# The second score matmul of two 64-wide attentions with 128 contraction rows instead of 64

## Chip, core and metric

The kernel runs on one core of a Trainium2 chip. Five engines work side by side, each through its own queue in a fixed order: TensorE (PE, with the weight loads PEld), VectorE (DVE), ScalarE (ACT), GpSimd (POOL) and SyncE (SP, which issues the DMAs here). The metric is the time of one execution on the device in microseconds (us), the median of several runs.

## What is computed

Three transformer blocks follow each other on one sequence of 1024 positions and width 1024, in float32. The change concerns the first and the third. The first block has differential attention with 4 heads; each head has two maps of width 64, a linear bias and a causal mask:

```python
scores = jnp.einsum('bhmqd,bhmkd->bhmqk', qblk, kt) + bias[None, :, None]
p = jax.nn.softmax(scores, axis=-1)
a = p[:, :, 0] - lam * p[:, :, 1]
return jnp.einsum('bhqk,bhkv->bhqv', a, vt)
```

Beside it runs a chunked retention, then an output projection and a feed-forward layer. The second block is convolutional and local. The third has attention over a window of 128 positions with 8 query heads of width 64, 2 key heads and a sink:

```python
s = jnp.einsum('bnqhgd,bnkhd->bnhgqk', qb, kw).astype(jnp.float32) * (D ** -0.5)
s = jnp.where(allowed[None, :, None, None], s, -jnp.inf)
p = jax.nn.softmax(jnp.concatenate([s, sink], axis=-1), axis=-1)[..., :-1]
```

and beside it a gated linear recurrence (HGRN2), cross-attention to a memory, and a convolutional feed-forward layer.

## The kernel before

**Number format.** PE multiplies in the format float32r, which keeps fewer bits than float32. So operands are split in a hi part, which ACT writes (`split`, L143), and a lo part, the rest, which DVE or POOL writes (L145). A product is three matmuls into one PSUM bank: hi x hi, hi x lo, lo x hi (`mm3`, L178 to L180). `dense` runs that over 8 slices of the contraction, 24 matmuls of 512 columns, `dense_tm` with 256 columns.

**Scores with width 64.** A contraction has 128 rows, a map only 64. The kernel uses that. For map m, `qs[m]` holds the query's hi part in the map's own 64 rows and its lo part in the other 64; `ks[m]` holds the key's hi part twice. One matmul with 128 rows then gives hi x hi + lo x hi. The term hi x lo is left: a second matmul into the same bank takes the 64 rows of `qs[m]` with the hi part, and the same 64 rows of `kl`, in which the lo parts of both maps lie one below the other. In the first block that pair is L539 and L540 in `attn_diff`, with operands from `proj_diff` (ACT writes at L458 and L463, DVE at L459 and L464, and four DMAs that carry parts to the other 64 rows). In the third block it is L1459 and L1460 in `window`, with operands from `stack`.

**First block, order of work.** For each head i: `attn_diff(i)`, the projections of the retention (`proj_ret`), the score operands of the next head (`proj_diff(i + 1)`), the retention (`attn_ret`), the next values (`proj_v`). Within `attn_diff`, pairs of 128 queries run over at most two column pieces of up to 512 keys: 24 score pairs a head. DVE adds the bias and takes the maximum (L544), ACT takes the exponential (L550), DVE combines both maps (L560), PE transposes (L568), ACT and DVE split the result (L570, L571), and PE multiplies by the values (`ps_o`). ACT copies that out (L576), and `finish` norms it: column sums on PE (L204), a power on POOL (L217), spreading on PE (L237).

**Third block.** There are 8 units, one for each of 4 head pairs and 2 halves of the sequence. In each, the steps of `core` (the recurrence: matmuls L1548, copies L1549, outputs L1559), of `window` (4 pieces of 128 queries, two heads each: 8 score pairs) and of the next unit's projections (`proj`) are interleaved.

**What sets the order.** Each engine's order is set when the kernel is built, by the framework's scheduler. It takes instructions in an order of its own from what their inputs, their tile buffers and its own estimates allow. PE then works strictly through the list. Most large tiles come from one pool of 37 slots (`SLOTS`, `e.slot`); a tile that finds no free slot waits until the last reader of an older one is done. PSUM banks are few: after `psum_split(d=2, s=3)` the attention has two for dense sums, three for scores, two for transposes and one for outputs (`ps_o`).

Of the kernel before, what the change touches and what calls it, by code (L numbers as in the profile page):

```python
# [10 lines left out]
F32 = mybir.dt.float32  # L11
F32R = mybir.dt.float32r
U8 = mybir.dt.uint8
AF = mybir.ActivationFunctionType
ALU = mybir.AluOpType
# [4 lines left out]
T = 1024  # L20
# [8 lines left out]
def half(h):  # L29
    return slice(h * HALF, h * HALF + HALF)  # L30


def blk(i, n=P):
    return slice(i * n, i * n + n)
# [325 lines left out]
def block1(e, next_gain):  # L360


    nc, tc, io = e.nc, e.tc, e.io
# [42 lines left out]
    with ExitStack() as c2:  # L406
# [38 lines left out]
        def proj_diff(hd):  # L445

            scale = 0.125 * 2.0 ** (2 * (hd + 1))
            ts = [e.slot("qk", (T,), F32R) for _ in range(5)]
            qs, ks, kl = ts[0:2], ts[2:4], ts[4]
            wq = e.chunk(io["w1_fm"][hd])  # L450
            wk = e.chunk(io["w1_fm"][4 + hd])
            for h in range(2):
                sl = half(h)
                ql = e.tsq(dt=F32R)
                p = normed(e.dense(wq, hs[h]), h)
                for m in range(2):
                    b = slice(64 * m, 64 * m + 64)
                    nc.scalar.activation(qs[m][b, sl], p[b], AF.Copy, scale=scale)  # L458
                    nc.vector.scalar_tensor_tensor(ql[b], p[b], scale, qs[m][b, sl].bitcast(F32), op0=ALU.mult, op1=ALU.subtract)  # L459
                p = normed(e.dense(wk, hs[h]), h)  # L460
                for m in range(2):
                    b = slice(64 * m, 64 * m + 64)
                    nc.scalar.activation(ks[m][b, sl], p[b], AF.Copy)  # L463
                    nc.vector.tensor_tensor(kl[b, sl], p[b], ks[m][b, sl].bitcast(F32), op=ALU.subtract)  # L464
                for m in range(2):
                    b = slice(64 * m, 64 * m + 64)
                    o = slice(64 - 64 * m, 128 - 64 * m)
                    nc.sync.dma_start(qs[m][o, sl].bitcast(F32), ql[b].bitcast(F32))
                    nc.sync.dma_start(ks[m][o, sl].bitcast(F32), ks[m][b, sl].bitcast(F32))
            return qs, ks, kl  # L470
# [47 lines left out]
        def attn_diff(hd, ops, v):  # L518
            qs, ks, kl = ops
            vh, vl = v  # L520
            slope = 2.0 ** (-2 * (hd + 1))
            for pr in range(4):
# [6 lines left out]
                for i in range(2):  # L529
                    qb = 2 * pr + i  # L530
                    sums = e.small.tile([P, 2, 2], F32, tag="sums", name="sums")
                    pm = []
                    for m in range(2):
                        mx = None
                        pc = []
                        for c, n in cols:
                            s = e.pss()[:, :n]
                            b = slice(64 * m, 64 * m + 64)
                            nc.tensor.matmul(s, lhsT=qs[m][:, blk(qb)], rhs=ks[m][:, c : c + n], start=True, stop=False)  # L539
                            nc.tensor.matmul(s, lhsT=qs[m][b, blk(qb)], rhs=kl[b, c : c + n], start=False, stop=True)  # L540
                            mx2 = e.small.tile([P, 1], F32, tag="mx", name="mx", bufs=8)
                            st = c - qb * P + 896
                            pt = pring.next()[:, :n]
                            nc.vector.tensor_tensor_reduce(  # L544
                                pt, s, strip[:, st : st + n], scale=-slope,
                                scalar=BIG if mx is None else mx, op0=ALU.add, op1=ALU.min, accum_out=mx2)
                            mx = mx2
                            pc.append(pt)
                        for j, pt in enumerate(pc):
                            nc.scalar.activation(pt, pt, AF.Exp, bias=mx, scale=-1.0, accum_out=sums[:, j, m : m + 1])  # L550
                        pm.append(pc)

                    if len(cols) == 2:
                        nc.vector.tensor_tensor(sums[:, 0], sums[:, 0], sums[:, 1], op=ALU.add)
                    rs = e.small.tile([P, 2], F32, tag="rs", name="rs")
                    nc.vector.reciprocal(rs, sums[:, 0])
                    nc.vector.tensor_copy(pre[:, qb % 4 : qb % 4 + 1], rs[:, 0:1])
                    nc.vector.scalar_tensor_tensor(rs[:, 1:2], rs[:, 1:2], nlam, sums[:, 0, 0:1], op0=ALU.mult, op1=ALU.mult)
                    for p0, p1 in zip(*pm):
                        nc.vector.scalar_tensor_tensor(p0, p1, rs[:, 1:2], p0, op0=ALU.mult, op1=ALU.add)  # L560
                    aa.append(pm[0])
# [759 lines left out]
def block3(e, acc, hs, rest, out):  # L1321
# [39 lines left out]
    with ExitStack() as c2:  # L1361
# [10 lines left out]
        def stack(w, scale, h, qs, kl=None):  # L1372

            p = e.dense(w, hs[h])
            ql = e.tsq(dt=F32R) if kl is None else kl
            for m in range(2):
                b = slice(64 * m, 64 * m + 64)
                o = slice(64 - 64 * m, 128 - 64 * m)
                nc.scalar.activation(qs[m][b], p[b], AF.Copy, scale=scale)
                nc.vector.scalar_tensor_tensor(ql[b], p[b], scale, qs[m][b].bitcast(F32), op0=ALU.mult, op1=ALU.subtract)  # L1380
                nc.sync.dma_start(qs[m][o].bitcast(F32), (ql[b] if kl is None else qs[m][b]).bitcast(F32))

        v = {}

# [30 lines left out]


        ks = [e.slot(f"k{m}", (T,), F32R) for m in range(2)]
        kl = e.slot("kl", (T,), F32R)
        va = e.slot("va", (8, P))

        def window_kv(h):
            stack(e.chunk(io["w3_fm"][4]), 1.0, h, [k[:, half(h)] for k in ks], kl[:, half(h)])
            p = e.dense(e.chunk(io["w3_fm"][5]), hs[h])
            t = e.tnt()
            nc.scalar.activation(t, p, AF.Copy)
            tp = e.pt()
            for b in range(4):
                nc.tensor.transpose(tp[:, blk(b)], t[:, blk(b)], e.ident)
            nc.vector.tensor_copy(va[:, 4 * h : 4 * h + 4], tp.rearrange("p (a b) -> p a b", a=4))
# [14 lines left out]
        def window(g, h):  # L1444
            qs = ops[g, h][4]
            po = e.po()
            for j4 in range(4):
# [7 lines left out]
                es = e.small.tile([P, 2], F32, tag="es2", name="es2")  # L1455
                pr = prring.next()
                for m in range(2):
                    b = slice(64 * m, 64 * m + 64)
                    nc.tensor.matmul(s[m], lhsT=qs[:, m, blk(j4)], rhs=ks[m][:, k0 : k0 + wd], start=True, stop=False)  # L1459
                    nc.tensor.matmul(s[m], lhsT=qs[b, m, blk(j4)], rhs=kl[b, k0 : k0 + wd], start=False, stop=True)  # L1460
                    nc.vector.tensor_tensor_reduce(pr[:, m, :wd], s[m], swm[:, w0:], scale=-1.0,
                                                   scalar=nsink[:, 2 * g + m : 2 * g + m + 1], op0=ALU.add, op1=ALU.min,
                                                   accum_out=mx[:, m : m + 1])
# [355 lines left out]
```

## Time and profile before

| | before |
|---|---|
| median of 3 runs | 3494.2 us (3491.73 to 3495.17) |
| profiled execution, its own time | 3490.75 us |
| its span, first to last instruction | 3489.0 us |
| PE busy | 3329.4 us, 95% of the span |
| weight loads (PEld) busy | 2737.6 us, 78% |
| DVE, ACT, POOL busy | 1922.8, 1348.9, 894.9 us |
| granted TensorE clock, mean | 0.974 |

An engine's busy time is the union of its instructions' spans. For PE the ends of matmuls are modelled and overlap the next, so the time from one start to the next tells more. The granted clock is the share of full speed that PE was given; it has two levels, 1.2 and 2.4 GHz, so 0.94 is a mean of time at both. In the lists of waits, an engine's idle time is put down to what came last.

### The profile page before, as it was taken

Reading aid. Unit: us, or ns where it says so; the run is one execution under the profiler, and the core shown is the slowest. Engines: PE = TensorE matmul, PEld = TensorE weight load, DVE = VectorE, ACT = ScalarE, POOL = GpSimd, SP = SyncE. Lnnn points to the kernel's source line nnn. Section 1 sums busy time; section 2 is a strip of 40 time slices with the busy share of each in tenths; the row PEclk is TensorE's granted clock in tenths of the full one; section 3 lists DMA queues with packets and bytes.
Section 4 is the critical chain, followed back from the end, with each engine's and each line's share of the span. In section 5 each row is a group of like instructions: output and inputs, shape, how many; then the busy total and the mean of one; then the engine's idle time right before and its main releaser. Section 6 shows DMA issues by size and latency. Waiting matters only on the chain.

```text
span 3489.0 us, 43291 instructions
## 1 busy us (share of the span) xinstructions
PE 3329.4 (95%) x16510; PEld 2737.6 (78%) x16510; DVE 1922.8 (55%) x3463; ACT 1348.9 (39%) x2354; POOL 894.9 (26%) x577
## 2 busy tenths in 40 slices
PE   7999998999999999889999899999899999999997
PEld 6788877888888887677667778878887788888886
DVE  8566566622222238984777575776635771434346
ACT  4444453412211233333544455554443442313132
POOL 2000013401100113521334444435333430202021
PEclk8999999999999999999999999999999999999999
DMA  4112123211111114345644221224423321111114
GB/s 126 46 44 59 49 77 125 94 58 43 46 53 53 43 60 139 115 120 164 204 153 133 74 68 58 82 85 151 151 67 103 133 93 57 47 53 44 53 42 146
DMA packets 122431, 306.23 MB, mean 88 GB/s; under 512 B 17008, under 2 KB 25584, under 8 KB 122224
## 3 DMA queue, kind: packets, MB, share of 16 engines
q1 hardware_dynamic: 122224, 303.47, 27.1%
q8 instruction: 130, 2.13, 0.3%
q14 instruction: 77, 0.63, 0.1%
HBM read 256.23 MB, written 40.37 MB: 85 GB/s over the span
## 4 chain that ended last, share of the span: by engine, by line
PE 38%; DVE 6%; issue 3%; ACT 2%; POOL 1%; DMA 0%; DVEq 0%; POOLq 0%; ACTq 0%
PE ps_d L178 11%; PE ps_d L180 11%; PE ps_d L179 11%; PE ps_s L1548 1%; ACT whi L143 1%; DVE act L145 1%; DVE ssum L263 0%; POOL wlo L145 0%; PE ps_o L1482 0%; PE ps_t L204 0%; DVE hSA L1549 0%; DVE pr L1124 0%; PE ps_s L1460 0%; DVE nq L272 0%; PE ps_d L1559 0%
## 5 line engine op out<-in xcount | busy, mean ns | idle before, releaser
L180 PE MATMUL ps_d<-act,wlo 128*128 128x512 f32 x2272 | 894.2, 394 | 14.5 <-DVE wlo L145 13.2
L178 PE MATMUL ps_d<-act,whi 128*128 128x512 f32 x2272 | 895.6, 395 | 8.0 <-ACT whi L143 4.3
L179 PE MATMUL ps_d<-act,whi 128*128 128x512 f32 x2272 | 895.9, 394 | 3.0 <-DVE act L145 3.0
L143 ACT ACTIVATE whi<-raw 128x1024 fp32r<-128x1024 f32 (+2 forms) x394 | 387.4, 984 | 969.9 <-PE ps_d L179 854.3
L145 POOL TENSOR_TENSOR wlo<-raw,whi 128x1024 fp32r<-128x1024 f32 (+1 forms) x162 | 391.9, 2422 | 740.1 <-ACT whi L143 714.2
L180 PEld LDWEIGHTS ps_d<-act,wlo 128*128 128x128 f32 x2272 | 429.8, 189 | 109.6 <-DVE wlo L145 17.1
L178 PEld LDWEIGHTS ps_d<-act,whi 128*128 128x128 f32 x2272 | 430.0, 189 | 103.3 <-ACT whi L143 9.2
L179 PEld LDWEIGHTS ps_d<-act,whi 128*128 128x128 f32 x2272 | 429.9, 189 | 98.9 <-issue 6.5
L145 DVE TENSOR_TENSOR wlo<-raw,whi 128x1024 fp32r<-128x1024 f32 (+2 forms) x232 | 259.1, 1117 | 276.5 <-ACT whi L143 276.0
L180 PE MATMUL ps_d<-up,wlo 128*128 128x512 f32 x864 | 336.5, 389 | 0.0
L179 PE MATMUL ps_d<-up,whi 128*128 128x512 f32 x864 | 336.2, 389 | 0.0
L178 PE MATMUL ps_d<-up,whi 128*128 128x512 f32 x864 | 335.5, 389 | 0.0
L686 POOL TENSOR_TENSOR nt<-sq 128x512 f32<-128x512 f32 x64 | 83.5, 1305 | 556.0 <-ACT sq L684 555.1
L180 PE MATMUL ps_d<-mix,wlo 128*128 128x512 f32 x512 | 202.6, 396 | 2.9 <-POOL wlo L145 2.9
L178 PE MATMUL ps_d<-mix,whi 128*128 128x512 f32 x512 | 201.1, 399 | 3.3 <-DVE acc L643 2.1
L179 PE MATMUL ps_d<-mix,whi 128*128 128x512 f32 x512 | 203.0, 397 | 0.0
L180 PEld LDWEIGHTS ps_d<-up,wlo 128*128 128x128 f32 x864 | 162.2, 188 | 34.0 <-DVE wlo L145 0.3
L179 PEld LDWEIGHTS ps_d<-up,whi 128*128 128x128 f32 x864 | 162.2, 188 | 33.8
L178 PEld LDWEIGHTS ps_d<-up,whi 128*128 128x128 f32 x864 | 162.2, 188 | 33.7
L693 DVE TENSOR_TENSOR acc<-ps_d,acc 128x512 f32<-128x512 f32 x96 | 66.4, 692 | 203.9 <-PE ps_d L180 203.9
L217 POOL TENSOR_TENSOR rr<-rv,mhalf 128x4 f32<-128x4 f32 (+1 forms) x43 | 45.8, 1065 | 486.3 <-DVE rv L211 274.6
L178 PE MATMUL ps_d<-whi,act 128*128 128x256 f32 x512 | 151.8, 299 | 19.4 <-ACT act L388 12.6
(404 smaller groups left out, 5528.5 us busy)
## 6 DMA issues: line engine op xcount, KB each, us to landing
raw<-in_w_up SPq DMA_DIRECT2D x94, 512.0 KB, 3.3
raw<-in_w_fm SPq DMA_DIRECT2D x84, 512.0 KB, 3.6
raw<-in_w_out SPq DMA_DIRECT2D x42, 512.0 KB, 3.3
raw<-in_w_down SPq DMA_DIRECT2D x64, 320.0 KB, 3.0
xd<-acc SPq DMA_DIRECT2D x64, 256.0 KB, 2.4
acc<-xd SPq DMA_DIRECT2D x64, 256.0 KB, 5.5
raw<-in_w_down SPq DMA_DIRECT2D x32, 384.0 KB, 3.2
raw<-in_w_tm SPq DMA_DIRECT2D x22, 512.0 KB, 3.3
```

The costliest lines, as they stand in the source:

```text
L143: nc.scalar.activation(hi, src, AF.Copy)
L145: e.tensor_tensor(lo, src, hi.bitcast(F32), op=ALU.subtract)
L178: nc.tensor.matmul(out, lhsT=wh, rhs=xh, start=start, stop=False)
L179: nc.tensor.matmul(out, lhsT=wh, rhs=xl, start=False, stop=False)
L180: nc.tensor.matmul(out, lhsT=wl, rhs=xh, start=False, stop=stop)
L217: self.nc.gpsimd.tensor_tensor(r, v, self.mhalf.broadcast_to([P, n]), op=ALU.pow)
L686: nc.gpsimd.tensor_tensor(u, r, r, op=ALU.mult)
L693: nc.vector.tensor_tensor(acc[f][:, h], p, acc[f][:, h], op=ALU.add)
L1548: nc.tensor.matmul(s[:, blk(j, 64)], lhsT=x[:, blk(j)], rhs=xv[:, nb * j : nb * j + nb, 1], start=True, stop=True)
```

## The change

The key's lo parts get a tile for each map. In `kl[m]` the map's own 64 rows hold the lo part as before, and the other 64 rows are set to zero by a memset on POOL. The second score matmul then takes all 128 rows of `qs[m]` and of `kl[m]`. What the query's lo rows add is multiplied by zero. Columns, PSUM banks and the number of matmuls stay. `proj_diff` takes 6 slots in place of 5 for each head, with two memsets; the third block takes one slot more for its whole length, and two memsets.

```diff
--- before.py
+++ after.py
@@ -445,8 +445,10 @@
         def proj_diff(hd):
 
             scale = 0.125 * 2.0 ** (2 * (hd + 1))
-            ts = [e.slot("qk", (T,), F32R) for _ in range(5)]
-            qs, ks, kl = ts[0:2], ts[2:4], ts[4]
+            ts = [e.slot("qk", (T,), F32R) for _ in range(6)]
+            qs, ks, kl = ts[0:2], ts[2:4], ts[4:6]
+            for m in range(2):
+                nc.gpsimd.memset(kl[m][64 - 64 * m : 128 - 64 * m].bitcast(F32), 0.0)
             wq = e.chunk(io["w1_fm"][hd])
             wk = e.chunk(io["w1_fm"][4 + hd])
             for h in range(2):
@@ -461,7 +463,7 @@
                 for m in range(2):
                     b = slice(64 * m, 64 * m + 64)
                     nc.scalar.activation(ks[m][b, sl], p[b], AF.Copy)
-                    nc.vector.tensor_tensor(kl[b, sl], p[b], ks[m][b, sl].bitcast(F32), op=ALU.subtract)
+                    nc.vector.tensor_tensor(kl[m][b, sl], p[b], ks[m][b, sl].bitcast(F32), op=ALU.subtract)
                 for m in range(2):
                     b = slice(64 * m, 64 * m + 64)
                     o = slice(64 - 64 * m, 128 - 64 * m)
@@ -535,9 +537,8 @@
                         pc = []
                         for c, n in cols:
                             s = e.pss()[:, :n]
-                            b = slice(64 * m, 64 * m + 64)
                             nc.tensor.matmul(s, lhsT=qs[m][:, blk(qb)], rhs=ks[m][:, c : c + n], start=True, stop=False)
-                            nc.tensor.matmul(s, lhsT=qs[m][b, blk(qb)], rhs=kl[b, c : c + n], start=False, stop=True)
+                            nc.tensor.matmul(s, lhsT=qs[m][:, blk(qb)], rhs=kl[m][:, c : c + n], start=False, stop=True)
                             mx2 = e.small.tile([P, 1], F32, tag="mx", name="mx", bufs=8)
                             st = c - qb * P + 896
                             pt = pring.next()[:, :n]
@@ -1372,13 +1373,15 @@
         def stack(w, scale, h, qs, kl=None):
 
             p = e.dense(w, hs[h])
-            ql = e.tsq(dt=F32R) if kl is None else kl
+            if kl is None:
+                ql = e.tsq(dt=F32R)
             for m in range(2):
                 b = slice(64 * m, 64 * m + 64)
                 o = slice(64 - 64 * m, 128 - 64 * m)
                 nc.scalar.activation(qs[m][b], p[b], AF.Copy, scale=scale)
-                nc.vector.scalar_tensor_tensor(ql[b], p[b], scale, qs[m][b].bitcast(F32), op0=ALU.mult, op1=ALU.subtract)
-                nc.sync.dma_start(qs[m][o].bitcast(F32), (ql[b] if kl is None else qs[m][b]).bitcast(F32))
+                lo = ql[b] if kl is None else kl[m][b]
+                nc.vector.scalar_tensor_tensor(lo, p[b], scale, qs[m][b].bitcast(F32), op0=ALU.mult, op1=ALU.subtract)
+                nc.sync.dma_start(qs[m][o].bitcast(F32), (lo if kl is None else qs[m][b]).bitcast(F32))
 
         v = {}
 
@@ -1415,11 +1418,13 @@
 
 
         ks = [e.slot(f"k{m}", (T,), F32R) for m in range(2)]
-        kl = e.slot("kl", (T,), F32R)
+        kl = [e.slot(f"kl{m}", (T,), F32R) for m in range(2)]
+        for m in range(2):
+            nc.gpsimd.memset(kl[m][64 - 64 * m : 128 - 64 * m].bitcast(F32), 0.0)
         va = e.slot("va", (8, P))
 
         def window_kv(h):
-            stack(e.chunk(io["w3_fm"][4]), 1.0, h, [k[:, half(h)] for k in ks], kl[:, half(h)])
+            stack(e.chunk(io["w3_fm"][4]), 1.0, h, [k[:, half(h)] for k in ks], [k[:, half(h)] for k in kl])
             p = e.dense(e.chunk(io["w3_fm"][5]), hs[h])
             t = e.tnt()
             nc.scalar.activation(t, p, AF.Copy)
@@ -1455,9 +1460,8 @@
                 es = e.small.tile([P, 2], F32, tag="es2", name="es2")
                 pr = prring.next()
                 for m in range(2):
-                    b = slice(64 * m, 64 * m + 64)
                     nc.tensor.matmul(s[m], lhsT=qs[:, m, blk(j4)], rhs=ks[m][:, k0 : k0 + wd], start=True, stop=False)
-                    nc.tensor.matmul(s[m], lhsT=qs[b, m, blk(j4)], rhs=kl[b, k0 : k0 + wd], start=False, stop=True)
+                    nc.tensor.matmul(s[m], lhsT=qs[:, m, blk(j4)], rhs=kl[m][:, k0 : k0 + wd], start=False, stop=True)
                     nc.vector.tensor_tensor_reduce(pr[:, m, :wd], s[m], swm[:, w0:], scale=-1.0,
                                                    scalar=nsink[:, 2 * g + m : 2 * g + m + 1], op0=ALU.add, op1=ALU.min,
                                                    accum_out=mx[:, m : m + 1])
```

The extra slot also changes the order. In the rows below, numbers of lines after L445 are 1 to 4 higher in the changed kernel (L576 is L577, L463 is L465).

PE at the end of head 1's attention, before: the last output matmuls (`ps_o`, 256 columns, with the values vh and vl), then dense work of the next head's key projection (`ps_d`).

```order
L178 MATMUL ps_o<-probT,vh 128x256
L179 MATMUL ps_o<-probT,vh 128x256
L180 MATMUL ps_o<-probT,vl 128x256
L179 MATMUL ps_d<-act,whi 128x512
L180 MATMUL ps_d<-act,wlo 128x512
L178 MATMUL ps_d<-act,whi 128x512
```

Seventeen such dense matmuls stand there, and the retention's output matmuls, which go to the same bank `ps_o`, come behind them.

PE at the same place in the changed kernel:

```order
L180 MATMUL ps_o<-probT,vl 128x256
L178 MATMUL ps_o<-probT,vh 128x512
L179 MATMUL ps_o<-probT,vh 128x512
L180 MATMUL ps_o<-probT,vl 128x512
L178 MATMUL ps_o<-probT,vh 128x384
L179 MATMUL ps_o<-probT,vh 128x384
L180 MATMUL ps_o<-probT,vl 128x384
L178 MATMUL ps_o<-probT,vh 128x256
L179 MATMUL ps_o<-probT,vh 128x256
L180 MATMUL ps_o<-probT,vl 128x256
L204 MATMUL ps_t<-ones_r,ssum 128x1 x4
L178 MATMUL ps_d<-act,whi 128x512
```

The retention's output matmuls (512, 384 and 256 columns) now follow the attention's directly, and the key projection's second half, all 24 of its matmuls, has moved behind the column sums L204. The same holds at the ends of heads 0 and 2.

ACT at that place, before (`probT` is the transposed or decayed weight, `o` the attention's output, `qk` a score operand):

```order
L458 ACTIVATE qk<-ps_d 64x512
L143 ACTIVATE probT<-prob 128x384
L143 ACTIVATE probT<-prob 128x256
L458 ACTIVATE qk<-ps_d 64x512
L576 ACTIVATE o<-ps_o 128x256
L259 ACTIVATE ssum<-o 128x512
L143 ACTIVATE whi<-raw 128x1024
L463 ACTIVATE qk<-ps_d 64x512 x2
```

ACT there in the changed kernel:

```order
L143 ACTIVATE probT<-prob 128x384
L143 ACTIVATE probT<-prob 128x256
L465 ACTIVATE qk<-ps_d 64x512
L577 ACTIVATE o<-ps_o 128x256
L460 ACTIVATE qk<-ps_d 64x512
L259 ACTIVATE ssum<-o 128x512
L143 ACTIVATE whi<-raw 128x1024
L465 ACTIVATE qk<-ps_d 64x512
L597 ACTIVATE prob<-ps_t,dec 128x128 x4
L465 ACTIVATE qk<-ps_d 64x512
```

Two of the writes of the next head's key tiles (L465) now stand behind the copy of the attention's output, because one of the six tiles takes the slot of this head's values.

POOL from the first block's start to the first retention, before (L145 splits the input, L217 is the power of a norm, L512 the retention's gate):

```order
L145 TENSOR_TENSOR act<-nq,act 128x512 x8
L217 TENSOR_TENSOR rr<-rv,mhalf 128x4 x3
L512 TENSOR_TENSOR nt<-nt,gate 128x512
L217 TENSOR_TENSOR rr<-rv,mhalf 128x4
L512 TENSOR_TENSOR nt<-nt,gate 128x512
```

POOL there in the changed kernel:

```order
L451 MEMSET qk 64x1024 x2
L145 TENSOR_TENSOR act<-nq,act 128x512 x8
L217 TENSOR_TENSOR rr<-rv,mhalf 128x4
L451 MEMSET qk 64x1024 x2
L217 TENSOR_TENSOR rr<-rv,mhalf 128x4 x2
L514 TENSOR_TENSOR nt<-nt,gate 128x512
```

Each head's two memsets stand ahead of work that was there before; those of head 1 wait for the last score matmul of head 0, whose operands lay in their slots.

## Rows read from the trace of the kernel before

**Rows 1.** Busy time of each engine, clock and DMA in three stretches

```profile
core 0: us, PE busy (x) PEld busy (x) DVE busy (x) ACT busy (x) POOL busy (x), PEclk, DMA share, GB/s
72.00:107.00 35.00, 32.82 (x113) 21.31 (x113) 30.03 (x74) 19.67 (x48) 6.51 (x4) 0.84 0.14 40
107.00:513.00 406.00, 405.34 (x2201) 330.39 (x2201) 237.17 (x598) 182.03 (x396) 26.75 (x22) 0.99 0.18 55
1946.00:2352.00 406.00, 381.62 (x2231) 315.85 (x2229) 274.42 (x649) 228.09 (x452) 181.56 (x154) 0.94 0.21 70
```

**Rows 2.** Timeline of PE, first block: start, duration (us), line, rows*columns loaded, output

```profile
89.08 0.40 PE L539 MATMUL ps_s<-qk 128*128 128x512 f32 x1
89.40 0.50 PE L540 MATMUL ps_s<-qk 64*128 64x512 f32 x1
89.83 0.50 PE L179 MATMUL ps_d<-act,whi 128*128 128x512 f32 x1
90.17 0.40 PE L180 MATMUL ps_d<-act,wlo 128*128 128x512 f32 x1
90.41 0.39 PE L178 MATMUL ps_d<-act,whi 128*128 128x512 f32 x1
90.64 0.40 PE L179 MATMUL ps_d<-act,whi 128*128 128x512 f32 x1
```

**Rows 3.** Timeline of PE, third block, around one score pair

```profile
2172.24 0.28 PE L1459 MATMUL ps_s<-k,swq 128*128 128x256 f32 x1
2172.44 0.38 PE L1460 MATMUL ps_s<-kl,swq 64*128 64x256 f32 x1
2172.75 0.50 PE L179 MATMUL ps_d<-act,whi 128*128 128x512 f32 x1
2173.09 0.39 PE L180 MATMUL ps_d<-act,wlo 128*128 128x512 f32 x1
```

**Rows 4.** Timeline of PE, two plain matmuls of 256 columns

```profile
175.02 0.28 PE L178 MATMUL ps_d<-whi,act 128*128 128x256 f32 x1
175.14 0.28 PE L179 MATMUL ps_d<-wlo,act 128*128 128x256 f32 x1
```

**Rows 5.** Timeline of the weight loads around rows 2, in brackets idle time before

```profile
89.40 0.18 PEld L540 LDWEIGHTS ps_s<-qk 64*128 64x128 f32 x1 [0.36 <-issue]
89.83 0.19 PEld L179 LDWEIGHTS ps_d<-act,whi 128*128 128x128 f32 x1 [0.25 <-issue]
90.17 0.19 PEld L178 LDWEIGHTS ps_d<-act,whi 128*128 128x128 f32 x1
```

**Rows 6.** One line's instructions: L540 in 107 to 513, L1460 in all

```profile
L540 PE MATMUL ps_s<-qk x79: 379/497/792, 107.2 to 510.3; 64*128 64x512 f32 x55, 64*128 64x256 f32 x24
...
L1460 PE MATMUL ps_s<-kl,swq x64: 323/380/579, 1946.6 to 2350.0; 64*128 64x256 f32 x56, 64*128 64x128 f32 x8
```

**Rows 7.** Waits of PE in 107 to 513, then 1946 to 2352: us, times, longest

```profile
PE ps_s L600 <- ACT prob L596: 0.7, 3, 0.2
...
PE ps_d L1559 <- DVE hSA L1549: 6.3, 6, 1.9
```

**Rows 8.** Waits of DVE in 72 to 107, then in 1946 to 2352

```profile
DVE prob L544 <- PE ps_s L540: 3.2, 3, 2.3
...
DVE rv L207 <- PE ps_t L204: 29.5, 7, 9.7
DVE hSA L1549 <- PE ps_s L1548: 19.3, 15, 3.4
DVE pr L1461 <- PE ps_s L1460: 18.4, 9, 4.9
```

**Rows 9.** Timeline of ACT at the end of head 1; POOL's memset of the second block

```profile
290.45 0.39 ACT L576 ACTIVATE o<-ps_o 128x256 f32<-128x256 f32 x1
...
L875 POOL MEMSET cb<- x2: 942/952/962, 1406.1 to 1419.1; 128x1024 f32 x2
```

## Prediction

> **What bounds the kernel now.** I read first the busy times by stretch, then TensorE's own instructions around one score pair, then who waited for whom. The two attentions that change lie in 72 to 513 us (first block) and in 1946 to 2352 us (third block). In [rows 1] TensorE (PE) is busy 405.3 of 406 us from 107 to 513, with the vector engine (DVE) at 237 us: nothing but PE limits that stretch. In 72 to 107 PE has 32.8 of 35 us, but DVE 30.0: both are near their limit. In 1946 to 2352 PE has 381.6 of 406 us, DVE 274.4, ACT 228.1, and the granted clock is 0.94, against 0.99 in the long stretch before.
>
> "Busy" hides the point, since a matmul's end is modelled; start-to-start times show it. In [rows 2] the first score matmul of a pair (L539, 128 rows, 512 columns) starts at 89.08, the second (L540, 64 rows) at 89.40, the next one with 128 rows at 89.83, the one after at 90.17 and two more at 90.41 and 90.64. So the intervals are 0.32, 0.43, 0.34, and then 0.24 and 0.23 between matmuls that all have 128 rows. The same at 256 columns in the third block is in [rows 3]: 0.20, 0.31, 0.34, where [rows 4] gives 0.12 from one 256-column matmul to the next. The weight loads tell why: the load for the 64-row matmul starts only with it, after 0.36 us in which the load path waits for nothing that the profile shows ("issue"), and so does the load of the next 128-row matmul (0.25); the load after that has no such gap [rows 5]. A change of the row count on PE, in either direction, thus stops the overlap of the next load with the running matmul.
>
> **The change, part by part.**
>
> *The second score matmul with 128 rows.* It has as many columns as before, and the number of columns sets PE's time: 0.23 us at 512, 0.12 at 256. Its extra rows multiply zeros. Both changes of row count beside each pair go. Per 512-column pair followed by a 512-column matmul: 0.32 + 0.43 + 0.34 = 1.09 becomes 3 x 0.23 = 0.69, a gain of 0.40 [rows 2]. Per 256-column pair: 0.20 + 0.31 + 0.34 = 0.85 becomes 0.12 + 0.12 + 0.23 = 0.47, a gain of 0.38 [rows 3, 4]. There are 79 pairs in 107 to 513 and 64 in the third block [rows 6], and 96 - 79 = 17 earlier (24 pairs a head, four heads).
>
> *107 to 513 us.* 79 x 0.40 = 31.6 us. What hides it? Nothing: PE waits 0.7 us for others in the whole stretch [rows 7], and DVE is at 58%. I take all of it.
>
> *72 to 107 us.* 17 x 0.40 = 6.8 us on PE, but DVE is idle only 5.0 of 35 us [rows 1], and of its idle time 3.2 us end with a score matmul [rows 8]. PE can give back no more than these 3.2 us; I take 2.
>
> *1946 to 2352 us.* 64 x 0.38 = 24.3 us on PE. Here PE already waits: 406 - 381.6 = 24.4 us, most of it at the end of each unit for DVE's last level of the recurrence (L1559, 6.3 us) [rows 7]. So a part of what PE saves turns into a longer wait. In the other direction DVE is idle 131.6 us, and the three largest rows in which it waited for PE make 67.2 us [rows 8], one half. The kept share lies between that half and all; two thirds, nearer to the rows, is 16 us.
>
> *The slots.* The pool has 37 slots. In the first block 16 hold the normalised input, 4 the values, 4 + 3 the two rings, 4 + 1 the retention's, 5 the score operands: 37. With six score operands it is 38, so one key tile of the next head waits for a value slot, which is free only after the last output matmul of the head before. The order shows what follows: the last half of the next head's key projection (24 matmuls) stands behind the column sums L204, where before 17 of them stood between the attention's last output matmuls and those of the retention. These share one PSUM bank, which the copy L576 empties. Before, the 17 dense matmuls hid that copy. Now the retention's matmuls wait for it: it starts at once where ACT is free, takes 0.39 us [rows 9], and with some 0.1 us before and after it costs about 0.6 us. The 24 matmuls that moved, 24 x 0.23 = 5.5 us, then cover the wait for the norm. With a little for the K tile that is emptied later, 1 us a head, three heads: 3 us. From below this is 0; from above it is one such half left without cover, 5.5 us a head, 16 us.
>
> *The memsets.* Ten, each of 64 x 1024. The trace has a memset of 128 x 1024 on GpSimd (POOL): 0.95 us [rows 9], so at most 0.95 each. POOL is busy 26.8 of 406 us in the long stretch [rows 1]. In its queue those of the next head stand ahead of a power for the norm (L217), but what they wait for is the last score matmul of the head before, and that head's last transposes and output matmuls lie between this one and the norm. Cost 0. The two in the third block stand before the split of an input half on POOL, at worst 1.9 us; I take 0, since PE has other work there.
>
> *Elsewhere.* PE's order is the same in the second block and in the third block's units up to the sixth; behind that a few pieces change places, which I cost at 0 with 2 us either way.
>
> *Sum.* 2 + 31.6 + 16 - 3 = 46.6 us. Against the profiled execution (3490.75 us; its span is 3489.0), 3444 us. That execution is 3.5 us below the median of the runs, which is within what these differ by.
>
> **The rivals.**
>
> *Third block bound by DVE and ACT (17%).* For it: its waits on DVE in [rows 7], POOL and ACT in the same chain. Against: DVE waits longer for PE than PE for DVE [rows 8]. Then only some 5 us of the 24.3 remain: 3455 us.
>
> *Everything kept (12%).* All 24.3 in the third block, 3.2 + 31.6 in the first, no new wait: 59 us, and 3 more if half of what 72 to 107 loses at its clock of 0.84 comes back (0.32 x 35 = 11.2 us at half clock lose 5.6): 3428 us. For it: DVE is nowhere over 86%.
>
> *The slots cost their upper bound (10%).* 16 us in place of 3: 3457 us. The place is the end of heads 0 to 2. Against: the order still gives PE 24 dense matmuls there.
>
> *No gain from PE (4%).* The gaps would stay if weight loads overlapped the running matmul only where its rows differ from those being loaded. The rows of plain 128-row matmuls speak against it: 0.23 to 0.24 us from start to start with a load of 0.19 in each [rows 2, 5]. If a load of 0.19 stayed open ahead of the second matmul and of the next one, 3 x 0.23 + 2 x 0.19 = 1.07 would replace the 1.09 of now [rows 2], 160 x 0.02 = 3 us: 3488 us. The Trainium skill, TensorE: Matmul & The Clock Gate, section The mechanism (Part 3), has that rule: loads overlap matmuls in flight only when the row group differs. By that rule the sum is 0 in place of 46.6; the trace disagrees, by the rows just named.
>
> *Slower (3%).* One mechanism: the granted clock. It is 0.94 in the third block [rows 1], which is 0.12 x 406 = 49 us at half clock (1.2 in place of 2.4 GHz), each losing half. The falls come where PE waits. If PE, with its work done sooner, waited more for DVE and fell back more often, each further us at half clock costs 0.5 us of PE's work. The gain of 46.6 is gone at 93 further us, and the kernel is slower by 0.2% (7 us) at 107. With half of the stretch, 203 us, at half clock: (203 - 49) / 2 = 77 us, and 3490.75 - 46.6 + 77 = 3521 us. Against: the waits that PE has now in place of the gaps would be no longer than the gaps are.
>
> **How the numbers follow.** The forecast, 3444 us, has 54%. The range takes in "everything kept" at its lower end (3428, with 2 us for the pieces that move, and 2 for how runs differ: 3424) and the two dearer cases up to both together (3455 + 13 = 3468): some 90% by my cases, and I count on one in ten that these miss something. What a measurement can tell from no change is 0.2%, 7 us. Faster by more: 54 + 17 + 12 + 10 = 93%. Within it: the case without gain, 4%. Slower: 3%.
>
> **What would show it.** In the profile of the changed kernel both score matmuls should have 128*128 rows, with 0.23 or 0.12 us from start to start and no "issue" row ahead of their loads. 107 to 513 should be some 28 us shorter with PE still at 99%; the unit ends in the third block should show L1559's wait grown from 6.3 to some 12 to 14 us, and the whole stretch 16 us shorter. Each end of a head should show one wait of 0.6 us of the retention's output matmuls for the copy of the attention's output. Wrong would be: a gap at the second score matmul that stays; a first block that gains less than 25 us, which would point to the slots; a clock in the third block under 0.9.

## The result, and the profile after

| | before | changed |
|---|---|---|
| median of 4 runs each | 3493.8 us (3491.73 to 3495.17) | 3454.9 us (3450.26 to 3462.76) |
| ratio, 95% interval | | 0.989 (0.987 to 0.991) |
| profiled execution, its own time | 3490.75 us | 3452.42 us |
| PE busy | 3329.4 us | 3271.2 us |

The changed kernel is 38.9 us faster, where 46.6 were forecast. In time, 3444 us was forecast, 11 us too low, with 3424 to 3468 as the range; 3 of these 11 us are the distance of the profiled execution, from which the forecast started, to the median of before. The score pairs are now L540 and L541 in the first block, L1463 and L1464 in the third.

Busy time of each engine in the stretches that answer to those of [rows 1], in the changed kernel:

```profile
core 0: us, PE busy (x) PEld busy (x) DVE busy (x) ACT busy (x) POOL busy (x), PEclk, DMA share, GB/s
...
71.00:100.00 29.00, 24.66 (x111) 19.11 (x112) 28.40 (x72) 18.12 (x42) 6.53 (x4) 0.91 0.18 50
99.00:478.00 379.00, 374.09 (x2214) 331.61 (x2213) 236.37 (x606) 183.41 (x402) 32.22 (x28) 1.00 0.19 59
1911.00:2314.00 403.00, 362.62 (x2234) 310.87 (x2235) 273.25 (x647) 227.91 (x452) 183.64 (x154) 0.93 0.22 71
```

406 us have become 379 in the first block (the edges are not quite the same work; the table below is exact on that), and DVE's 237 us of work is unchanged. The third block is still 403 us, with PE busy 19 us less of it. So PE has its gain in both, and only the first block hands it on.

The gain on PE itself is about as forecast. Timeline of PE in the first block, which answers to [rows 2]:

```profile
84.48 0.40 PE L540 MATMUL ps_s<-qk 128*128 128x512 f32 x1
84.71 0.39 PE L541 MATMUL ps_s<-qk 128*128 128x512 f32 x1
84.94 0.39 PE L179 MATMUL ps_d<-act,whi 128*128 128x512 f32 x1
85.17 0.39 PE L180 MATMUL ps_d<-act,wlo 128*128 128x512 f32 x1
```

Timeline of the weight loads at pairs a little later, which answers to [rows 5]:

```profile
88.73 0.19 PEld L540 LDWEIGHTS ps_s<-qk 128*128 128x128 f32 x1
88.96 0.19 PEld L541 LDWEIGHTS ps_s<-qk 128*128 128x128 f32 x1
89.19 0.19 PEld L540 LDWEIGHTS ps_s<-qk 128*128 128x128 f32 x1
```

All starts are 0.23 us apart (0.32, 0.43 and 0.34 before), and no load has a gap ahead of it. In the third block (PE):

```profile
2143.65 0.28 PE L1464 MATMUL ps_s<-kl,swq 128*128 128x256 f32 x1
2143.77 0.29 PE L178 MATMUL ps_d<-whi,act 128*128 128x256 f32 x1
2143.89 0.28 PE L179 MATMUL ps_d<-wlo,act 128*128 128x256 f32 x1
```

Over all pairs outside half clock (the time at the lower of the clock's two levels), the time that the three intervals of a pair take beyond plain 128-row matmuls (each excess counted up to 0.35 us) fell from 0.455 to 0.04 us in the first block and from 0.445 to 0.09 in the third: 96 x 0.415 = 40 us and 64 x 0.35 = 22 us.

Where this went was read by laying two traces over each other: for each instruction the difference of its start in both (the same rank among those of its line), and at a mark the median over the instructions within 4 us. The steps between marks, in us of gain against the trace of before; the marks are times of before:

| kernel | 72 to 107 | 107 to 513 | 513 to 560 | 560 to 1946 | 1946 to 2352 |
|---|---|---|---|---|---|
| changed, three traces | 4.4, 4.0, 4.4 | 30.3, 30.4, 28.8 | -3.2, -3.2, -1.5 | 2.0, -4.7, 0.4 | 3.4, 3.2, -0.2 |
| e1, e9: rows alone, order as before | 4.4, 4.4 | 33.0, 33.1 | -2.7, -2.1 | -0.7, 3.8 | 6.7, 9.7 |
| e2, e11: third block's extra tile outside the slots | 4.4, 4.0 | 28.7, 30.4 | -3.4, -3.0 | -1.9, -1.2 | 8.1, 9.6 |
| e4: first block alone | 4.4 | 28.7 | -1.9 | -0.4 | 1.5 |
| e6: third block alone, rows alone | 0.5 | 0.0 | -2.4 | 2.5 | 7.2 |
| e3: tiles and slots, 64 rows | -0.1 | -2.2 | 0.1 | 2.7 | -5.1 |
| e7: before again | 0.5 | 0.0 | 0.3 | -1.5 | -1.5 |

Between 560 and 1946 the code is the same in all of them, and still the steps run from -4.7 to 3.8: one profile tells nothing about a term of that size. The records show the granted clock falling at other moments in each execution, and one program can be at half clock for 181 us in all (before) or for 195 (e7). So single profiles decide a term only where several agree. The row of the changed kernel adds up to 33 us (mean of its three traces), where the medians of its runs give 38.9, 37.1 and 32.8 us.

### The profile page after: what moved, and what is told of

The parts are those of the page before. It is cut to its first block, busy times and chain, and to the rows that moved or that the text cites. A ratio compares the mean times of both kernels' runs of the same rounds, so it can differ in the third digit from the quotient of the medians.

```text
span 3450.6 us, 43309 instructions
## 1 busy us (share of the span) xinstructions
PE 3271.2 (95%) x16510; PEld 2733.1 (79%) x16510; DVE 1921.5 (56%) x3463; ACT 1346.7 (39%) x2354; POOL 908.2 (26%) x587
## 4 chain that ended last, share of the span: by engine, by line
PE 75%; DVE 14%; issue 4%; ACT 4%; DMA 1%; POOL 1%; SPq 0%; DVEq 0%; ACTq 0%; POOLq 0%
PE ps_d L178 22%; PE ps_d L179 22%; PE ps_d L180 22%; DVE ca L887 2%; ACT whi L143 1%; DVE wlo L145 1%; DVE act L145 1%; PE ps_t L204 1%; DVE ssum L263 1%; POOL wlo L145 1%; DVE nq L272 1%; DVE acc L1270 1%; PE ps_t L237 0%; PE ps_o L1135 0%; PE ps_t L1128 0%
## 5 line engine op out<-in xcount | busy, mean ns | idle before, releaser
L145 POOL TENSOR_TENSOR wlo<-raw,whi 128x1024 fp32r<-128x1024 f32 (+1 forms) x162 | 392.6, 2427 | 745.4 <-ACT whi L143 690.2
L145 DVE TENSOR_TENSOR wlo<-raw,whi 128x1024 fp32r<-128x1024 f32 (+2 forms) x232 | 259.6, 1119 | 279.5 <-ACT whi L143 278.9
L179 PE MATMUL ps_d<-wlo,act 128*128 128x256 f32 x512 | 151.3, 298 | 2.7 <-POOL wlo L145 1.6
```

What stands on the lines that cost most here:

```text
L145: e.tensor_tensor(lo, src, hi.bitcast(F32), op=ALU.subtract)
L179: nc.tensor.matmul(out, lhsT=wh, rhs=xl, start=False, stop=False)
```

## The experiments

**Rows alone (e1, e9).** With kl left as one tile, the second matmul can still take all 128 rows: the other 64 rows of kl then hold the other map's lo parts, and what is added is the query's lo part times the other map's key lo part: no term of the product, but an error of the size of the lo x lo that the kernel leaves out.

```diff
-                            nc.tensor.matmul(s, lhsT=qs[m][b, blk(qb)], rhs=kl[b, c : c + n], start=False, stop=True)
+                            nc.tensor.matmul(s, lhsT=qs[m][:, blk(qb)], rhs=kl[:, c : c + n], start=False, stop=True)
```

and the same in `window`. No slot, no memset, and each engine's order is that of before, instruction for instruction.

> Both score matmuls take 128 rows, but kl stays the one tile of before, with the lo parts of both maps one below the other: no sixth slot, no memset, the order of every engine as before. (In place of zero rows the second matmul adds the query's lo part times the other map's key lo part, a term of the size of the lo x lo product that the kernel leaves out anyway.) So the number of rows alone changes. Theory R (row count sets PE's gaps, and the third block lost its gain to the order that the extra slot brings): first block about 36 us, third block about 14, together 50: 3444 us (3438 to 3450). Rival B (the third block is bound by the vector engine and ACT whatever the order): first block 36, third 4: 3454 us. Rival O (the gain of the changed kernel came from its order): 3494 us.

Measured: 3447.4 us against 3490.0 of before on that chip, ratio 0.988 (0.987 to 0.989). The times expected for e1 to e4 start from 3494 us, so gains are compared here and below. The gain is PE's row count and not the order, so rival O falls. With 42.6 us it lies between R (50) and B (40), nearer to B: from 72 to 560 the first block gives 35 us, about as both said, and the third 7, where R said 14 and B 4. PE's waits in the third block, in e1:

```profile
PE ps_d L1557 <- DVE hSA L1547: 8.1, 7, 2.6
...
PE ps_t L237 <- DVE diag L231: 1.8, 1, 1.8
```

All its waits make 31.5 us there, against 24.3 before; L1557 is the L1559 of [rows 7].

**The third block's extra tile in a pool of its own (e2, e11).**

```diff
-        kl = [e.slot(f"kl{m}", (T,), F32R) for m in range(2)]
+        kl = [e.slot("kl0", (T,), F32R), odd.tile([P, T], F32R, name="kl1")]
```

> The changed kernel with the third block's second key tile taken from a pool of its own in place of one of the 37 slots; first block as in the changed kernel. The third block's order is then that of before but for two memsets. Theory R: the 6.2 us wait of the norm's spreading matmul L237 behind L231 at 2227 to 2233 goes, the 24 dense matmuls stand again between L204 and L237, and the third block keeps some 9 us more: 3446 us. Rival B: 3455 us, as the changed kernel.

Measured: ratio 0.989 (0.988 to 0.991), 3452.2 us, a gain of 37.7 us where R gave 48 and B 39. By the median alone B would stand. The traces show a part of R: the wait of L237 is 1.8 us again, and the third block gained 8.1 us (9.6 in e11), on average 6.7 us more than in the three traces of the changed kernel; R had said some 9.

**Tiles, slots and memsets with 64 rows (e3).**

```diff
-                            nc.tensor.matmul(s, lhsT=qs[m][:, blk(qb)], rhs=kl[m][:, c : c + n], start=False, stop=True)
+                            b = slice(64 * m, 64 * m + 64)
+                            nc.tensor.matmul(s, lhsT=qs[m][b, blk(qb)], rhs=kl[m][b, c : c + n], start=False, stop=True)
```

and the same in `window`. The order is that of the changed kernel but for some 30 places of PE's 16510 matmuls.

> The changed kernel's tiles, slots and memsets, but the second score matmul with 64 rows again: what slots and order cost without the gain. Theory R: about 3 us in the first block (three ends of heads) and 6 to 9 us in the third (the wait at the end of unit 5): 3503 us (3500 to 3507). If slots and order cost nothing: 3494 us. Upper bound of the prediction for the first block's slots, 16 us, and the third block's 8: 3518 us.

Measured: 3494.8 us, ratio 1.0017 (1.0008 to 1.0026), 4.8 us slower than before on that chip, about half of the 9 that R said. Its trace has both costs: 2.2 us in 107 to 513, and 7.5 us between 2155 and 2290, the end of unit 5. The wait of PE for the norm in its third block:

```profile
PE ps_t L237 <- DVE diag L231: 8.0, 2, 6.2
```

In the rest of the third block it gained 2.4 us on the trace of before, which it should not; differences of that size stand between two profiles of one program too (e7's row).

**First block alone (e4).** `stack`, `window` and the tiles of the third block as before, `proj_diff` and `attn_diff` as changed.

> The change in the first block alone, the third as before. Theory R: 32 us of gain by the end of the first block, and nothing behind it: 3462 us. If the drift seen in the second block of the changed kernel (2 us further gain) belongs to the change: 3460 us.

Measured: 3459.8 us, ratio 0.991 (0.990 to 0.993), 30.2 us faster, where 32 were expected. Behind 560 us no step is clear of the differences named above, so the trace shows nothing of the change that acts behind its place.

**The changed kernel again (e5), the third block alone (e6), before again (e7).** e6 is the edit of e1 in `window` only.

> The changed kernel again, beside the next ones on one chip, for a second profile of it. Theory R (slots and order cost 3 us in the first block and 7 in the third; the order-neutral kernel was at 0.9878 of before): 0.9878 x 3490 + 10 = 3457 us on such a chip, ratio 0.990 to 0.991, with the 6 us wait of L237 at the end of unit 5 again and a first block shorter by 32 us. If the slots cost less than the trace says: 3450 us, ratio 0.9885.

> 128 rows for the second score matmul in the third block alone, with the one stacked kl tile, so that every engine's order is as before (a term of the size of the left-out lo x lo product is added, as in the first experiment); first block as before. TensorE's gaps fall by 64 x 0.35 = 22 us. If PE bounds the third block: 22 us faster, ratio 0.9937. If most of it turns into waits for the vector engine and into half clock, as the first experiment's trace suggests: 5 to 9 us, ratio 0.9975 to 0.9985, PE's waits in the block 31 to 33 us in place of 24.

> The kernel of before again, for a second profile of it on the chip of these runs: 3490 us, half clock in the third block 41 to 51 us, as in the three traces with its code there. If the half clock differs as much between profiles of one program as between the programs, the granted clock explains no difference in the third block.

Measured: e5 3453.1 us, ratio 0.990 (0.989 to 0.992), its trace with the same wait of 6.2 us. e6 3482.5 us, 0.998 (0.997 to 0.999): 7.8 us faster, where PE's gaps shrank by 22. e7 3489.4 us, 1.000 (0.999 to 1.001). The three ratios are as expected; e7's half clock (58.0 us, expected 41 to 51) is not. From the first to the last score pair the records show half clock for 51.2, 41.0, 58.0 and 47.8 us in the four traces with the third block of before (before, e4, e7, e8), and for 64.9, 51.2, 61.4, 54.6 and 54.6 us in the five with 128 rows in the old order (e1, e9, e6, e2, e11). The means are 49.5 and 57.3, but one program differs by 7 us between two executions (before, e7) and another by 14 (e1, e9). By the rule set ahead of e7 the clock then explains no difference here: that it takes some 4 us (half of the difference of the means) is possible and not shown.

**Both score matmuls with 64 rows (e8).** In the first block, `qs[m][b, ...]` and `ks[m][b, ...]` in the first matmul of the pair too.

```diff
-                            nc.tensor.matmul(s, lhsT=qs[m][:, blk(qb)], rhs=ks[m][:, c : c + n], start=True, stop=False)
+                            nc.tensor.matmul(s, lhsT=qs[m][b, blk(qb)], rhs=ks[m][b, c : c + n], start=True, stop=False)
```

> The kernel of before with 64 rows for both score matmuls in the first block (the query's lo part times the key's hi part is left out). The number of row changes per pair stays two, one into the pair and one out of it. Theory R (a change of the row count costs): the interval from the first to the second matmul of a pair falls to 0.23 us, the excess per pair stays near 0.4 us and the time near 3490 us. Rival (a matmul with 64 rows is itself slow, or loads never overlap one with the same rows): 0.43 us also within the pair, 0.2 us more per pair, 96 pairs: 3509 us. The order of PE moves a little, so the intervals count more than the total.

Measured: 3473.7 us, ratio 0.996 (0.994 to 0.997), faster by 16.5 us, which neither said. PE's timeline shows two pairs in a row:

```profile
131.97 0.50 PE L539 MATMUL ps_s<-qk 64*128 64x512 f32 x1
132.31 0.40 PE L540 MATMUL ps_s<-qk 64*128 64x512 f32 x1
132.55 0.39 PE L539 MATMUL ps_s<-qk 64*128 64x512 f32 x1
132.79 0.39 PE L540 MATMUL ps_s<-qk 64*128 64x512 f32 x1
133.11 0.50 PE L179 MATMUL ps_d<-act,whi 128*128 128x512 f32 x1
133.44 0.40 PE L180 MATMUL ps_d<-act,wlo 128*128 128x512 f32 x1
```

The weight loads in the same stretch:

```profile
131.97 0.18 PEld L539 LDWEIGHTS ps_s<-qk 64*128 64x128 f32 x1 [0.24 <-issue]
132.08 0.18 PEld L540 LDWEIGHTS ps_s<-qk 64*128 64x128 f32 x1
132.31 0.18 PEld L539 LDWEIGHTS ps_s<-qk 64*128 64x128 f32 x1
...
133.11 0.19 PEld L179 LDWEIGHTS ps_d<-act,whi 128*128 128x128 f32 x1 [0.37 <-issue]
```

From 132.31 to 132.79 matmuls with 64 rows follow each other at 0.24 us: 64 rows are not slow, and the loads at 132.08 and 132.31 run under a matmul with as many rows. The change is slow: only the loads at a change (131.97 and 133.11) start with their own matmul, and the interval that ends with it and the one after it are 0.1 us longer each (0.32 and 0.33 at the way out). Medians of the time from the start of a 512-column matmul ("this") to the start of the next, outside half clock, in 72 to 513 us (e8: to 500):

| rows of the one before, this, the next | trace | count | median ns |
|---|---|---|---|
| 128, 128, 128 | before | 839 | 227 |
| 128, 128, 64 | before | 49 | 322 |
| 128, 64, 128 | before | 45 | 428 |
| 64, 128, 128 | before | 38 | 337 |
| 128, 64, 64 | e8 | 35 | 336 |
| 64, 64, 128 | e8 | 38 | 323 |
| 64, 64, then 64 and 128 | e8 | 11 | 234 |

An interval with a change at one side has 0.1 us more, with a change at both sides 0.2. A lone pair keeps two changes and its cost of 0.4 us, as expected; its inner interval was expected at 0.23 us and is 0.34, since the change ahead of it still shows there. Pairs that stand side by side share theirs, which before they could not. The rest of the 16.5 us is in the section on the hardware. The Trainium skill, TensorEngine Tiling (Array Packing), section Key Properties, says that a change of the tiling mode drains the engine. The traces fit that, at 0.2 us a change; the drain itself is in no row.

**All three on one chip (e9, e10, e11).**

> The order-neutral form again (128 rows in both score matmuls, one stacked kl tile, a term of the size of the left-out lo x lo product added), beside the changed kernel on one chip. From the traces: 2.9 us for the first block's slots and 4 to 5 us for the third block's order, so 7 to 8 us under the changed kernel: ratio to before 0.988, changed kernel 0.990. If slots and order cost nothing by the median: both alike within 2 us.

> The changed kernel, beside the two others on one chip: ratio 0.990 (0.989 and 0.9903 so far), third block 400.5 us from its first to its last score pair, as in its two traces, with the 6 us wait of L237.

> The changed kernel with the third block's second key tile in a pool of its own: third block 396 us from first to last score pair (395.6 in its trace) against 400.5 of the changed kernel, so 4 us less than that in all: ratio 0.989, and 3 us more than the stacked form, for the first block's slots. If the third block's order costs nothing by the median: as the changed kernel.

Measured, against 3489.3 us of before: rows alone 3446.6 us (0.988, 0.986 to 0.990), tile outside the slots 3450.3 (0.988, 0.987 to 0.990), changed kernel 3456.5 (0.990, 0.988 to 0.992). They stand in the expected order; the distances to the changed kernel, 9.9 and 6.2 us, are a little above the expected 7 to 8 and 4, and the intervals of the ratios overlap. The earlier runs (3447.4, 3452.2 and 3453.1 us, on two chips whose kernels of before differ by 0.2 us) give 5.7 and 0.9 us. From first to last score pair the third block took 403.8 us in the changed kernel (400.5 expected) and 394.0 with the tile outside the slots (396). Rows alone has the lowest median both times. It needs neither slot nor memset, at the price of the added error terms. Over all runs, seven of eight of rows alone lie under 3451 us and one of fourteen of the changed kernel; so it is likely the faster one, though the intervals of each pair overlap.

## Why the prediction came out as it did

**The mechanism was right.** The change of the row count stopped the loads from overlapping (e8's loads above), the zero rows cost nothing, and both intervals are at 0.23 and 0.12 us. The rival without a gain is gone: 1065 intervals of 512 columns in the changed kernel's first block, each with the load of the next 128 rows in it, have a median of 227 ns. The rule of the Trainium skill that gave that rival (TensorE: Matmul & The Clock Gate, The mechanism) does not agree with these rows.

By the median the gain is 7.7 us short of the forecast. By the traces the stretches miss by +2.3, +1.2, -2.6 and -13.9 us in the order of the table; so the others and the spread of the executions hide a part of the third block's error, and the time is better than its terms.

**107 to 513, with the slots: 28.6 forecast, 29.8 measured** (mean of three traces). Without the slots it is 33.0 (31.6 forecast), so these cost 3.2; 3 was forecast, but by a wrong working, so that this fits is luck. PE and ACT at the end of head 1 in the changed kernel, first PE, then ACT:

```profile
268.30 0.28 PE L180 MATMUL ps_o<-probT,vl 128*128 128x256 f32 x1
270.30 0.50 PE L178 MATMUL ps_o<-probT,vh 128*128 128x512 f32 x1 [1.71 <-ACT o L577]
```

```profile
268.40 0.82 ACT L143 ACTIVATE probT<-prob 128x384 fp32r<-128x384 f32 x2
269.25 0.59 ACT L465 ACTIVATE qk<-ps_d 64x512 fp32r<-64x512 f32 x1
269.86 0.38 ACT L577 ACTIVATE o<-ps_o 128x256 f32<-128x256 f32 x1
```

The copy does not start "at once where ACT is free": ACT is at splits and at a write of the next head's key (L465), which stand ahead in its queue. PE waits 1.7 us and not 0.6:

```profile
PE ps_o L178 <- ACT o L577: 4.9, 3, 1.7
```

That line is the only one in PE's waits from 99 to 478, and e3, with the same 4.9 us, lost 2.2 net. So some 2 us of the waits are given back later, where I had put 0.4 a head on top.

**72 to 107: 2 forecast, 4.3 measured.** I allowed PE only the idle time of DVE that ended with a score matmul (3.2 us). DVE is now busy 28.4 of 29 us, so nearly all its idle time went, whatever had ended it. DVE became the limit where I said, only later.

**513 to 560: nothing forecast, 2.6 us lost.** In all eight traces whose first block has 128 rows, 10.2 to 13.7 us there are at half clock, against 3.4 us in before, e3, e7 and e8 and 6.8 in e6. The stretch in before, and then in the changed kernel (the clock is the third number from the end):

```profile
505.00:560.00 55.00, 46.36 (x232) 36.66 (x232) 35.51 (x70) 28.20 (x56) 19.15 (x13) 0.97 0.35 116
```

```profile
470.00:528.00 58.00, 48.81 (x238) 39.74 (x237) 37.86 (x73) 29.08 (x57) 19.65 (x13) 0.91 0.37 118
```

The clock is 0.91 in place of 0.97. e6, with the first block as before but 6.8 us at half clock, lost 2.4 us there too, which speaks for the clock as the cause. Why a faster first block is followed by more of it is open.

**1946 to 2352: 16 forecast, 2.1 measured.** This is the step that failed, in two of its parts.

*The kept share.* Of 24.3 us I kept two thirds, because DVE waited longer for PE than PE for DVE. With the order of before, five traces keep 8.3 us on average (6.7 to 9.7) of the measured 22: a bit over a third. PE's waits rose from 24.6 (mean of before, e4 and e7) to 32.4 us (mean of the five): 7.8 us. Only 1.7 of these are at L1559, the place named ahead; 4.0 stand ahead of the recurrence's other matmuls (L1548), 1.8 of them for POOL's `hE`, and 1.4 ahead of the window's transposes (L1477). Nor did L1559 make most of PE's waits before, as I wrote, but a quarter (6.3 of 24.3). Kept gain and waits make 16 of the 22 us; the half clock may have some 4 more, which is not shown. The rival "third block bound by DVE and ACT" said 5 us; it was nearer than my choice. DVE's waits for PE in [rows 8] were no measure of what DVE could give, since the largest of the three did not shrink. The same rows in e1:

```profile
DVE rv L207 <- PE ps_t L204: 31.6, 6, 9.3
DVE pr L1459 <- PE ps_s L1458: 15.1, 7, 4.4
DVE hSA L1547 <- PE ps_s L1546: 11.2, 10, 2.6
```

Between the same two groups of traces the wait for the column sums (L204) went from 30.0 to 31.2 us; the other two fell by 11.4 us together (18.3 to 14.7 and 18.7 to 10.8). Why the first stays is open.

*"A few pieces change places, which I cost at 0 with 2 us either way."* They cost 6 us (8.3 less 2.1). With one slot fewer, the scheduler puts the 24 dense matmuls of the next projection, at the end of unit 5, ahead of the column sums L204 and not between L204 and L237. (The steps of the memory's norm, L1294, take slots too; whether the slot acts through them is not shown.) PE there, before:

```profile
2264.18 0.95 PE L204 MATMUL ps_t<-ones_r,ssum 128*128 128x1 f32 x8
2264.99 0.49 PE L179 MATMUL ps_d<-act,whi 128*128 128x512 f32 x1
...
2270.12 0.39 PE L180 MATMUL ps_d<-act,wlo 128*128 128x512 f32 x1
2270.34 0.39 PE L237 MATMUL ps_t<-diag,ones_r 128*128 128x512 f32 x1
```

PE in the changed kernel:

```profile
2225.28 0.39 PE L180 MATMUL ps_d<-act,wlo 128*128 128x512 f32 x1
...
2226.18 1.05 PE L204 MATMUL ps_t<-ones_r,ssum 128*128 128x1 f32 x8
2233.42 0.80 PE L237 MATMUL ps_t<-diag,ones_r 128*128 128x512 f32 x1 [6.18 <-DVE diag L231]
```

DVE in the same stretch:

```profile
2228.22 0.87 DVE L1294 SCALAR_TENSOR_TENSOR nt<-mem,g_mem_norm,ps_t 128x256 f32<-128x256 f32 x2
2229.01 0.15 DVE L207 TENSOR_SCALAR rv<-ps_t 128x4 f32<-128x4 f32 x1
...
2232.39 0.17 DVE L225 CAST rh<-rr 128x4 fp32r<-128x4 f32 x1 [0.56 <-POOL rr L217]
```

POOL there, in the changed kernel and then before:

```profile
2228.87 2.34 POOL L145 TENSOR_TENSOR wlo<-raw,whi 128x1024 fp32r<-128x1024 f32 x1 [6.01 <-ACT whi L143]
2231.17 1.19 POOL L217 TENSOR_TENSOR rr<-rv,mhalf 128x4 f32<-128x4 f32 x1
```

```profile
2265.40 1.01 POOL L217 TENSOR_TENSOR rr<-rv,mhalf 128x4 f32<-128x4 f32 x1 [4.96 <-DVE rv L207]
2266.38 2.39 POOL L145 TENSOR_TENSOR wlo<-raw,whi 128x1024 fp32r<-128x1024 f32 x1
```

Before, 5 us of dense work covered the norm's way through DVE and POOL (L207, L217, L225, L231); now nothing does. Two things stand in the way: DVE starts L207 1.8 us after L204's end (2227.23), behind work of the memory's norm (L1294), and POOL starts L217 2.0 us after L207's end, behind a split of a weight (L145) that stood behind L217 before. The wait has the same 6.2 us in all three traces of the changed kernel and in e3, with that split ahead of L217 in all four, and is 1.8 us in each trace with the third block's order of before, e2 among them, which differs from the changed kernel by the place of that one tile. In before:

```profile
PE ps_t L237 <- DVE diag L231: 1.8, 1, 1.8
```

Between 2155 and 2290 the changed kernel loses 6.7, 6.7 and 5.2 us. PE's waits in its third block, which answer to [rows 7]:

```profile
PE ps_d L1563 <- DVE hSA L1553: 9.2, 7, 2.6
PE ps_t L237 <- DVE diag L231: 8.0, 2, 6.2
```

I had expected L1559 to rise to 12 to 14 us; it is 9.2, and the larger loss stood in the row below.

**The other rivals.** "Everything kept" is right for the first block alone. The slots never came near their upper bound of 16 us. The clock did not turn the result: 0.93 in the third block against 0.94. The memsets are off the path: 0.95 us each, as costed.

## What to carry to other kernels

Between 128-row matmuls, a matmul with 64 rows was dearer here than one filled up with zeros: each change of the row count cost 0.2 us, so try to fill the rows up, or to put matmuls of one shape side by side. What PE saves counts in full only in the stretch where nothing else waits: split the gain by stretch, and take little where PE itself already waits. And an extra tile in a full pool has a price of its own, which is read from the order: at each place where pieces change, ask which work stood between a producer and the one who waits for it.

## What the hardware showed beside this

Matmuls of 64 rows in different halves of the array run side by side. In e8, where map 0 uses one half and map 1 the other, PE's timeline has groups of two that start almost together (22 intervals between two such matmuls are under 60 ns, 21 of them 5 to 10 ns):

```profile
188.94 0.28 PE L180 MATMUL ps_d<-whi,act 128*128 128x256 f32 x1
189.15 0.39 PE L539 MATMUL ps_s<-qk 64*128 64x256 f32 x2
189.37 0.28 PE L540 MATMUL ps_s<-qk 64*128 64x256 f32 x2
189.58 0.39 PE L178 MATMUL ps_d<-whi,act 128*128 128x256 f32 x1
189.81 0.28 PE L179 MATMUL ps_d<-wlo,act 128*128 128x256 f32 x1
```

From 188.94 to 189.81 six matmuls of 256 columns take 0.87 us, with both changes of the row count; six plain ones take 0.72, and with 0.4 for the changes it would be 1.12 without the overlap. The Trainium skill, TensorE: Matmul & The Clock Gate, section Why this matters for your kernels, has small contractions in distinct row groups running concurrently, with starts up to 4 ns apart; this trace agrees on the concurrency, its starts are a little further apart. That and the shared changes are what the trace shows behind e8's 16.5 us; how much is whose was not separated, and PE's order moves a little too.
